# Weight factors of two up-projection blocks, made during the output projection and kept in DRAM; right factors made product by product

## The chip, the cores and the metric

The kernel runs on one core of one Trainium2 chip. The time is the device time of one execution, in microseconds; a kernel's time is the median of its runs.

## The reference

One layer of a hybrid decoder over 2048 tokens of width 1024, all in float32. A pooling mixer and a sliding-window attention are gated, added and projected by w_out onto the residual stream. Then comes the feed-forward part, which is what matters here:

```python
x = x + (g_pool * a + g_attn * b) @ w_out[l]
h = rmsnorm(x, ffn_norm[l])
up = causal_depthwise_conv(h @ w_up[l], conv_w[l], conv_b[l])   # 1024 -> 2 * 2816, width 3
gate, val = up[..., :D_FF], up[..., D_FF:]
x = x + (jax.nn.silu(gate) * val) @ w_down[l]
```

## The kernel before

**Halves and stages.** The tokens are worked in two halves (c = 0 and 1) of 1024. In each half come the mixer and the attention, the output projection (out_proj), the up-projection (up) with convolution and gate, and the down-projection. TensorE has no float32 product of its own here: each operand is split into a high part (a cast, on ScalarE) and a low part (a subtraction, on VectorE), and three matmuls (high x high, high x low, low x high) are added up in PSUM. mm3 does that for the projections, product for the up-projection.

**Up-projection.** There are 22 blocks f. A block is 128 gate columns and 128 value columns of w_up, and the whole is a 2x2 matrix of halves: gate and value against the two halves of the 1024 inputs on the left, inputs against the two halves (512) of the tokens on the right. It is multiplied by the scheme of Strassen and Winograd with seven products: A11 B11 (one), A12 B21 (two), S2 T2 (three), S1 T1 (four), S3 T3 (five), S4 B22 (six) and A22 T4 (seven). Each has 12 matmuls of 128 x 512 (four slices of the inputs, three parts). Up holds one block; its methods one to seven write the products into PSUM banks (tags f, a, t) and put them together: ScalarE copies a bank out (kept, tile Q) where a later one is added to it on VectorE.

**Left factors.** Blocks makes those of one block from its raw weights, in four steps: first gives A11 and A12, second A22, third S3 and S2, fourth S1 and S4, each by VectorE sums in place, a cast and a low part (L262 on VectorE and L261 on ScalarE for a full tile). The raw weights come through Stream, which loads three entries ahead of use (tiles R, three buffers) and parts the entry after next. w_out goes through the same Stream (L191 and L192 part its slabs), 16 slabs for two passes n over the token halves, and then the 22 blocks of w_up.

**Right factors.** xg holds x2 scaled by the norm's weight, in four tiles. The norm's own factor for a token half is known only when the squares of all eight row groups have been summed (rstd, L461 to L471), raised to a power on POOL (L464) and spread over the partitions (L480, L482). Half 0 is normed within the projection's second pass, and right_first makes B11 and B21 there. Half 1 is normed only in the up-projection's head: right_rest norms it (L865), forms the differences in place (L876 for T1, L882 for T2, L886 for T3, L889 for T4) and parts each factor (parted: L805 cast, L806 low part).

**Order.** The program is written as in the listing, but a scheduler places each instruction by its priority and by when its operands are ready, so engines work across these steps. SP issues all transfers from one queue in order. Buffers are few: tiles U 19, M 5, F 4, Q 4, R 3. In the head of up the order was: products one of blocks 0 and 1, spread, two of block 0, one of block 2, right_rest, two of blocks 1 and 2, then the loop over f, in which a block's products three to five are followed by six and seven of the block before.

Of the kernel before, what the change touches and what calls it, by code (L numbers as in the profile page):

```python
# [16 lines left out]
F32 = mybir.dt.float32  # L17
# [9 lines left out]
P = 128  # L27
# [16 lines left out]
MAGIC = 12582912.0  # L44
FOLD_FIRST = 5


# [77 lines left out]
def weight_order():  # L125
    out = []
    for c in range(NCH):
        if c > 0:
            out.append(("kv",))
        out += [(kind, j) for parts in first_fillers(c) for kind, j, n in parts if n == 0]  # L130
        out.append(("q", 0))
        for q4 in range(4):
            for n, parts in enumerate(fillers(c, q4)):
                if n == NB - 3 and q4 < 3:
                    out.append(("q", q4 + 1))
                out += [(kind, j) for kind, j, h in parts if h == 0]
        out += [("pg", ct) for ct in (6, 7)]
        out += [("out", m) for n in range(2) for m in range(KT)]
        out += [("up", f) for f in range(FT)]
        out += [("none", i) for i in range(3)]  # L140
    return out
# [23 lines left out]
def block_kernel(ctx: ExitStack, tc: tile.TileContext, x, xT, pos, vec, qkn, w_poolT, w_pool, w_q, w_kv,  # L165
# [66 lines left out]
    def split_weights(key, raws):  # L232
# [14 lines left out]
        return out if len(out) > 1 else out[0]  # L247

    class Blocks:

# [5 lines left out]
        def __init__(self, raws):  # L256
            self.raws, self.w, self.at = raws, {}, 0

        def halved(self, first, second, raw):
            t = up_.tile([P, 2, 8, P], F32R, "U")  # L260
            A.copy(t[:, 0], raw)  # L261
            V.tensor_sub(t[:, 1], raw, t[:, 0].bitcast(F32))  # L262
            self.w[first], self.w[second] = t[:, :, 0:4], t[:, :, 4:8]
# [10 lines left out]
        def second(self):  # L274
            g, v = self.raws
            t = mp.tile([P, 2, 4, P], F32R, "M")
            A.copy(t[:, 0], v[:, 4:8])
            V.tensor_sub(t[:, 1], v[:, 4:8], t[:, 0].bitcast(F32))
            self.w["A22"] = t
            V.tensor_sub(v[:, 0:4], g[:, 0:4], v[:, 0:4])  # L280
            V.tensor_sub(v[:, 4:8], v[:, 4:8], v[:, 0:4])  # L281
# [533 lines left out]
    def out_proj(c, ms):  # L815

        xg = [up_.tile([P, 2, T], F32, "U") for _ in range(4)]
        norms = []
        for n in range(2):
            acc = fp.tile([P, 512], F32, "F")  # L820
            c_ = slice(n * 512, (n + 1) * 512)
            for m in range(KT):
                xr = fp.tile([P, 512], F32, "F")
                load(xr, xT[m * P:(m + 1) * P, c * T + n * 512:c * T + (n + 1) * 512])
                w = stream.get("out", m)
                if n == 1 and m == 7:
                    stream.ahead().step(4)
                    stream.part(stream.used + 2)
                    stream.tiles[stream.used + 1].step(1)
                po = ps.tile([P, 512], F32, "f")  # L830
# [25 lines left out]
            norms += [stats, whole]  # L856
        return xg, b, norms[2:]

# [12 lines left out]

    def right_rest(xg, b, pb):
        for j in range(2):
            normed(xg[j], 1, pb)
            q11, q12 = xg[j][:, :, N0], xg[j][:, :, N1]
            V.tensor_sub(q11, q12, q11)  # L876
            b.setdefault("T1", []).append(parted(q11))
        t2s = []
        for j in range(2):
            normed(xg[j + 2], 1, pb)  # L880
            t2s.append(mp.tile([P, 2, 512], F32, "M"))
            V.tensor_sub(t2s[j], xg[j + 2][:, :, N1], xg[j][:, :, N0])  # L882
            b.setdefault("T2", []).append(parted(t2s[j]))
        for j in range(2):
            q12, q21, q22 = xg[j][:, :, N1], xg[j + 2][:, :, N0], xg[j + 2][:, :, N1]
            V.tensor_sub(q12, q22, q12)  # L886
            b.setdefault("T3", []).append(parted(q12))
            b.setdefault("B22", []).append(parted(q22))
            V.tensor_sub(q21, q21, t2s[j])  # L889
            b.setdefault("T4", []).append(parted(q21))  # L890
# [12 lines left out]
    class Up:  # L903
# [27 lines left out]

        def four(self):
            self.z = ps.tile([P, 512], F32, "t")
            self.mul(self.z, "S1", "T1", first=True)
# [33 lines left out]

        def gate(self):
            yg = self.conv(self.f, self.ug)  # L970
            t = mp.tile([P, T], F32, "M")
# [4 lines left out]

    def up(c, xg, b, norms, dn):
        units = [Up(c, f, b, None) for f in range(FT)]

# [6 lines left out]

        weights(0, 4)
        units[0].one()
        norms[0]()
        weights(1, 1)  # L990
        units[1].one()
        pb = norms[1]()
        units[0].two()
        weights(2, 1)
        units[2].one("t")
        right_rest(xg, b, pb)
        units[1].two()
        units[2].two()
        for f in range(FT + 1):
            u = units[f] if f < FT else None  # L1000
            old = units[f - 1] if f > 0 else None
            if u and f > 2:
# [6 lines left out]
            weights(f + 1, 1)  # L1009
            if old:  # L1010
                old.seven()
                old.value()
            weights(f + 1, 1)
            if f == 0:
                u.four()
            if u:
# [3 lines left out]
            weights(f + 1, 1)  # L1020
            if old:
                old.six()
                old.gate()
            weights(f + 1, 1)
            if f > 0 and u:
                u.four()
            if u:
                u.five()
# [296 lines left out]
```

## Time and profile before

| | |
|---|---|
| runs | 2494.67, 2495.66, 2496.61 us; median 2495.66 |
| the profiled execution | 2497.94 us, its span 2495.9, granted clock 0.995 |
| TensorE busy | 98% of the span |
| VectorE, ScalarE, POOL busy | 79%, 48%, 9% |
| DMA | 229.86 MB, 92 GB/s over the span |
| first half: output projection, head of up, block 2 on | from about 538, 624.4, 666.6 us |
| second half: head of up | from 1843.7 us |

The span is what the profile covers; the 2.0 us by which the execution's time exceeds it lie around it. Rows of the profile name engines as PE (TensorE matmul), PEld (its weight loads), DVE (VectorE), ACT (ScalarE), POOL and SP; L865 is line 865 of the listing. out<-in gives the names of the tiles without their numbers. The granted clock (PEclk) is 1.00 at 2.4 GHz and 0.50 at 1.2 GHz.

### The profile page before, as it was taken

Reading aid. Unit: us, or ns where it says so; the run is one execution under the profiler, and the core shown is the slowest. Engines: PE = TensorE matmul, PEld = TensorE weight load, DVE = VectorE, ACT = ScalarE, POOL = GpSimd, SP = SyncE. Lnnn points to the kernel's source line nnn. Section 1 sums busy time; section 2 is a strip of 40 time slices with the busy share of each in tenths; the row PEclk is TensorE's granted clock in tenths of the full one; section 3 lists DMA queues with packets and bytes.
Section 4 is the critical chain, followed back from the end, with each engine's and each line's share of the span. In section 5 each row is a group of like instructions: output and inputs, shape, how many; then the busy total and the mean of one; then the engine's idle time right before and its main releaser. Section 6 shows DMA issues by size and latency. Waiting matters only on the chain.

```text
span 2495.9 us, 32928 instructions
## 1 busy us (share of the span) xinstructions
PE 2438.3 (98%) x12224; PEld 2056.6 (82%) x12224; DVE 1982.5 (79%) x3544; ACT 1189.0 (48%) x2350; POOL 223.5 (9%) x217
## 2 busy tenths in 40 slices
PE   6999999999999999999999999999999999999999
PEld 6888888878788888788889888887877888887887
DVE  8786777876988788799857767779589788788994
ACT  6444444544554555543524444444445555454432
POOL 0121222200000000000002322222000000000000
PEclk9999999999999999999999999999999999999999
DMA  6221111035122233445221011100522222218321
GB/s 244 98 85 35 35 43 43 26 97 169 64 85 91 78 110 118 165 173 185 92 103 35 26 43 43 43 26 26 186 93 85 85 76 90 88 68 278 122 82 51
DMA packets 86991, 229.86 MB, mean 92 GB/s; under 512 B 9264, under 2 KB 11568, under 8 KB 86832
## 3 DMA queue, kind: packets, MB, share of 16 engines
q1 hardware_dynamic: 86832, 227.77, 26.8%
q8 instruction: 96, 1.57, 0.3%
q14 instruction: 63, 0.52, 0.1%
HBM read 183.69 MB, written 44.04 MB: 91 GB/s over the span
## 4 chain that ended last, share of the span: by engine, by line
PE 77%; DVE 14%; issue 3%; ACT 3%; DMA 2%; POOL 0%; SPq 0%; POOLq 0%; DVEq 0%; ACTq 0%
PE f L207 19%; PE f L896 17%; PE t L896 9%; PE a L207 6%; PE f L1166 4%; PE a L1166 4%; PE a L896 4%; PE s L1166 4%; PE t L1166 4%; DVE U L806 1%; ACT Q L677 1%; PE a L710 1%; PE s L656 1%; DVE F L760 1%; DVE U L192 1%
## 5 line engine op out<-in xcount | busy, mean ns | idle before, releaser
L207 PE MATMUL f<-U,U 128*128 128x512 f32 x3072 | 719.3, 391 | 7.4 <-ACT U L191 4.2
L207 PEld LDWEIGHTS f<-U,U 128*128 128x128 f32 x3072 | 570.6, 188 | 127.1 <-ACT U L191 6.7
L896 PE MATMUL f<-U,U 128*128 128x512 f32 x1512 | 366.4, 393 | 7.0 <-ACT U L805 2.3
L896 PEld LDWEIGHTS f<-U,U 128*128 128x128 f32 x1512 | 285.8, 189 | 71.4 <-ACT U L805 4.4
L962 DVE SCALAR_TENSOR_TENSOR M<-F,vc,M 128x1024 f32<-128x1024 f32 x176 | 225.1, 1282 | 130.5 <-ACT M L959 130.2
L896 PE MATMUL t<-U,U 128*128 128x512 f32 x1128 | 268.3, 391 | 2.9 <-ACT U L805 2.6
L207 PE MATMUL a<-U,U 128*128 128x256 f32 x1920 | 250.0, 286 | 14.1 <-ACT U L191 12.2
L207 PEld LDWEIGHTS a<-U,U 128*128 128x128 f32 x1920 | 242.9, 193 | 21.6 <-ACT U L191 12.2
L896 PEld LDWEIGHTS t<-U,U 128*128 128x128 f32 x1128 | 211.7, 188 | 50.2 <-ACT U L805 4.1
L677 ACT ACTIVATE Q<-s,st,r 128x128 f32<-128x128 f32 x256 | 114.3, 453 | 175.4 <-DVE st L672 167.6
L261 ACT CAST U<-R 128x1024 fp32r<-128x1024 f32 x132 | 137.9, 1054 | 64.8 <-DVE R L281 32.7
L569 POOL TENSOR_TENSOR r<-r,mhalf 128x4 f32<-128x4 f32 (+1 forms) x80 | 77.2, 966 | 950.0 <-DVE r L568 888.3
L262 DVE TENSOR_TENSOR U<-R,U 128x1024 fp32r<-128x1024 f32 x132 | 161.0, 1222 | 0.0
L192 DVE TENSOR_TENSOR U<-R,U 128x512 fp32r<-128x512 f32 x214 | 146.2, 712 | 16.8 <-ACT U L191 15.8
L191 ACT CAST U<-R 128x512 fp32r<-128x512 f32 x214 | 123.0, 619 | 42.6 <-PE f L207 27.2
L896 PE MATMUL a<-U,U 128*128 128x512 f32 x528 | 128.4, 390 | 0.0
L896 PE MATMUL f<-U,M 128*128 128x512 f32 x504 | 123.6, 394 | 3.7 <-DVE F L940 3.7
L1125 ACT CAST U<-U 128x1024 fp32r<-128x1024 f32 x74 | 77.2, 1051 | 86.2 <-PE a L1166 27.2
L896 PEld LDWEIGHTS f<-U,M 128*128 128x128 f32 x504 | 95.5, 190 | 24.9 <-DVE F L940 5.0
L896 PEld LDWEIGHTS a<-U,U 128*128 128x128 f32 x528 | 98.7, 188 | 20.3
L948 ACT COPY F<-f 128x512 f32<-128x512 f32 x42 | 24.8, 590 | 179.1 <-PE f L896 179.1
L959 ACT ACTIVATE M<-F,vc 128x1024 f32<-128x1024 f32 x88 | 109.3, 1244 | 1.3
(243 smaller groups left out, 3903.3 us busy)
## 6 DMA issues: line engine op xcount, KB each, us to landing
R<-w_up SPq DMA_DIRECT2D x88, 512.0 KB, 3.3
actd<-M SPq DMA_DIRECT2D x44, 512.0 KB, 2.6
U<-w_down SPq DMA_DIRECT2D x88, 256.0 KB, 5.3
U<-actd SPq DMA_DIRECT2D x88, 256.0 KB, 5.4
R<-w_out SPq DMA_DIRECT2D x32, 512.0 KB, 3.9
R<-w_ga SPq DMA_DIRECT2D x16, 512.0 KB, 3.3
R<-w_q SPq DMA_DIRECT2D x16, 512.0 KB, 3.3
R<-wfold SPq DMA_DIRECT2D x16, 512.0 KB, 3.3
```

The lines of the kernel that those rows point to most:

```text
L191: A.copy(hi[:, t], src[:, t])
L192: V.tensor_sub(lo[:, t], src[:, t], hi[:, t].bitcast(F32))
L207: nc.tensor.matmul(out, a, b, start=(i == 0), stop=(i == n - 1))
L261: A.copy(t[:, 0], raw)
L262: V.tensor_sub(t[:, 1], raw, t[:, 0].bitcast(F32))
L569: G.tensor_tensor(r, r, mhalf[:, 0:nh], op=ALU.pow)
L677: A.activation(pr[:, h, :], sc[:, h, 0:P], AF.Exp, bias=nm[:, h:h + 1], scale=it["rq"][:, h:h + 1], accum_out=rs[:, h:h + 1])
L896: nc.tensor.matmul(bank, a[:, x, k, :], b[k // 2][:, y, k % 2, :], start=(first and i == 0), stop=(i == 11), skip_group_check=True)
L959: A.activation(y, u[:, 2:], AF.Identity, bias=cw[:, 3, m:m + 1], scale=cw[:, 2, m:m + 1])
L962: V.scalar_tensor_tensor(y, u[:, j:j + T], cw[:, j, m:m + 1], y, op0=ALU.mult, op1=ALU.add)
L1125: A.copy(hi, src)
L1166: nc.tensor.matmul(into[m], u[:, 0, c_], v[:, 1], start=(first and j == 0), stop=(k == n - 1 and j == 2), skip_group_check=True)
```

## The change

Blocks 0 and 1 (PRE, with the row groups 0 and 4 at which they begin) leave the Stream. In the first pass of the first output projection their raw weights are loaded into a tile U, and Blocks makes all four of their tiles there, two steps at each of the next two row groups; at the third, store writes the tiles (high and low parts, 3.5 MiB a block) to DRAM. In the head of up of both halves the new class Kept loads these tiles back: A11 and A12 in the second pass of the output projection, the others at the points given in up. So the second half makes no left factors of these two blocks at all. right_rest is cut into right_t1, right_t2, right_t3, right_b22 and right_t4, which up calls in this order between the products: one of blocks 0, 1; two of 0, one of 2 (T1), two of 1 and 2 (T2), four of 0 (T3), three of 0, four of 1 (B22), five of 0 (T4), six and seven of 0, three and five of 1. The loop over f begins with block 2.

```diff
+PRE = {0: 0, 1: 4}
+
+
 V_AN = 0
...
         out += [("out", m) for n in range(2) for m in range(KT)]
-        out += [("up", f) for f in range(FT)]
+        out += [("up", f) for f in range(FT) if f not in PRE]
         out += [("none", i) for i in range(3)]
...
+    kept = {}
+
+    class Kept:
+
+
+        def __init__(self, f):
+            self.f, self.w = f, {}
+
+        def fetch(self, *names):
+            i = PARTS.index(names)
+            src = kept[self.f][i]
+            p, tag = (mp, "M") if names == ("A22",) else (up_, "U")
+            t = p.tile(list(src.shape), F32R, tag)
+            load(t.bitcast(F32), src)
+            for j, name in enumerate(names):
+                self.w[name] = t[:, :, 4 * j:4 * j + 4]
+
+        def step(self, n=1):
+            pass
+
+    PARTS = [("A11", "A12"), ("A22",), ("S3", "S2"), ("S1", "S4")]
+
     class Blocks:
...
             self.raws, self.w, self.at = raws, {}, 0
+            self.tiles = []
+
+        def store(self, f):
+            kept[f] = []
+            for i, t in enumerate(self.tiles):
+                kept[f].append(dp.tile(list(t.shape), F32, f"kept_{f}_{i}"))
+                load(kept[f][-1], t.bitcast(F32))
...
             t = up_.tile([P, 2, 8, P], F32R, "U")
+            self.tiles.append(t)
             A.copy(t[:, 0], raw)
...
             self.w["A22"] = t
+            self.tiles.append(t)
             V.tensor_sub(v[:, 0:4], g[:, 0:4], v[:, 0:4])
...
         norms = []
+        heads = [Kept(f) for f in PRE]
         for n in range(2):
...
                 w = stream.get("out", m)
+                for f, at in PRE.items() if c == n == 0 else ():
+                    if m == at:
+                        raw = up_.tile([P, 2, 8, P], F32, "U")
+                        load(raw[:, 0], w_up[f])
+                        load(raw[:, 1], w_up[FT + f])
+                        made = Blocks([raw[:, 0], raw[:, 1]])
+                    elif at < m < at + 3:
+                        made.step(2)
+                    elif m == at + 3:
+                        made.store(f)
+                if n == 1 and m >= 6:
+                    heads[m - 6].fetch("A11", "A12")
                 if n == 1 and m == 7:
-                    stream.ahead().step(4)
-                    stream.part(stream.used + 2)
-                    stream.tiles[stream.used + 1].step(1)
+                    stream.ahead().step(1)
                 po = ps.tile([P, 512], F32, "f")
...
             norms += [stats, whole]
-        return xg, b, norms[2:]
+        return xg, b, norms[2:], heads
...
-    def right_rest(xg, b, pb):
+    def right_t1(xg, b, pb):
         for j in range(2):
...
             b.setdefault("T1", []).append(parted(q11))
+
+    def right_t2(xg, b, pb):
+
         t2s = []
...
             b.setdefault("T2", []).append(parted(t2s[j]))
+        return t2s
+
+    def right_t3(xg, b):
         for j in range(2):
-            q12, q21, q22 = xg[j][:, :, N1], xg[j + 2][:, :, N0], xg[j + 2][:, :, N1]
+            q12, q22 = xg[j][:, :, N1], xg[j + 2][:, :, N1]
             V.tensor_sub(q12, q22, q12)
             b.setdefault("T3", []).append(parted(q12))
-            b.setdefault("B22", []).append(parted(q22))
+
+    def right_b22(xg, b):
+        for j in range(2):
+            b.setdefault("B22", []).append(parted(xg[j + 2][:, :, N1]))
+
+    def right_t4(xg, b, t2s):
+        for j in range(2):
+            q21 = xg[j + 2][:, :, N0]
             V.tensor_sub(q21, q21, t2s[j])
...
-        def four(self):
-            self.z = ps.tile([P, 512], F32, "t")
+        def four(self, tag="t"):
+            self.z = ps.tile([P, 512], F32, tag)
             self.mul(self.z, "S1", "T1", first=True)
...
-        def gate(self):
-            yg = self.conv(self.f, self.ug)
+        def gate(self, yg=None):
+            if yg is None:
+                yg = self.conv(self.f, self.ug)
             t = mp.tile([P, T], F32, "M")
...
-    def up(c, xg, b, norms, dn):
-        units = [Up(c, f, b, None) for f in range(FT)]
+    def up(c, xg, b, norms, heads, dn):
+        units = [Up(c, f, b, heads[f] if f < 2 else None) for f in range(FT)]
...
-        weights(0, 4)
-        units[0].one()
+
+        u0, u1, u2 = units[:3]
+        u0.one()
         norms[0]()
-        weights(1, 1)
-        units[1].one()
+        u1.one()
         pb = norms[1]()
-        units[0].two()
+        u0.two()
+        weights(2, 0)
+        u2.one("t")
+        for u in (u0, u1):
+            u.w.fetch("S1", "S4")
+        u0.w.fetch("S3", "S2")
+        right_t1(xg, b, pb)
+        u1.two()
+        u2.two()
+        t2s = right_t2(xg, b, pb)
+        u0.four()
+        u0.w.fetch("A22")
+        right_t3(xg, b)
+        u0.three()
+        u1.four("a")
+        right_b22(xg, b)
+        u0.five()
+        u1.w.fetch("S3", "S2")
+        right_t4(xg, b, t2s)
         weights(2, 1)
-        units[2].one("t")
-        right_rest(xg, b, pb)
-        units[1].two()
-        units[2].two()
-        for f in range(FT + 1):
+        u0.six()
+        yg = u0.conv(0, u0.ug)
+        u0.seven()
+        u0.value()
+        weights(2, 1)
+        u1.w.fetch("A22")
+        u1.three()
+        u0.gate(yg)
+        weights(2, 1)
+        u1.five()
+        for f in range(2, FT + 1):
             u = units[f] if f < FT else None
-            old = units[f - 1] if f > 0 else None
+            old = units[f - 1]
             if u and f > 2:
...
             weights(f + 1, 1)
-            if old:
-                old.seven()
-                old.value()
+            old.seven()
+            old.value()
             weights(f + 1, 1)
-            if f == 0:
-                u.four()
             if u:
...
             weights(f + 1, 1)
-            if old:
-                old.six()
-                old.gate()
+            old.six()
+            old.gate()
             weights(f + 1, 1)
-            if f > 0 and u:
+            if u:
                 u.four()
-            if u:
                 u.five()
```

On SP the four stores of block 0 stand among the stores of x2 of row groups 1 to 3 of the first pass, and those of block 1 among groups 5 to 7; behind block 0's stand loads of xT and w_out and the raw weights of block 1. In the head of the first half the loads run: A11/A12 of block 0, the gate part of block 3's w_up, x2, A11/A12 of block 1, S1/S4 of 0, x2, S1/S4 of 1, S3/S2 of 0, A22 of 0, S3/S2 of 1, A22 of 1, then the value part of block 3.

The first place is VectorE in the head of the first half, from the statistics of token half 1 (r, L461 before, L495 now) on; R is raw weights, s the spread factor, U_5845 to U_5848 are xg. Before:

```order
L461 TENSOR_SCALAR r_15_204<-a_6574 128x4
L280 TENSOR_TENSOR R_6501<-R_6499,R_6501 128x512
L480 COPY M_6612<-r_15_204 128x512
L278 TENSOR_TENSOR M_6589<-R_6501,M_6589 128x512
L281 TENSOR_TENSOR R_6501<-R_6501 128x512
L288 TENSOR_TENSOR R_6499<-R_6499,R_6501 128x512
L289 TENSOR_TENSOR R_6499<-R_6499,R_6501 128x512
L865 TENSOR_TENSOR U_5845<-U_5845,s_6611 128x2x512
L926 TENSOR_TENSOR F_6557<-a_6618,Q_6572 128x512
L262 TENSOR_TENSOR U_6636<-R_6553,U_6636 128x1024
L876 TENSOR_TENSOR U_5845<-U_5845 128x2x512
L865 TENSOR_TENSOR U_5846<-U_5846,s_6611 128x2x512
```

Now, from the same place on:

```order
L495 TENSOR_SCALAR r_15_204<-a_6612 128x4
L514 COPY M_6641<-r_15_204 128x512
L910 TENSOR_TENSOR U_5845<-U_5845,s_6640 128x2x512
L910 TENSOR_TENSOR U_5846<-U_5846,s_6640 128x2x512
L921 TENSOR_TENSOR U_5845<-U_5845 128x2x512
L984 TENSOR_TENSOR F_6595<-a_6647,Q_6610 128x512
L921 TENSOR_TENSOR U_5846<-U_5846 128x2x512
L840 TENSOR_TENSOR U_6690<-U_5845,U_6690 128x1024
L910 TENSOR_TENSOR U_5847<-U_5847,s_6640 128x2x512
L840 TENSOR_TENSOR U_6695<-U_5846,U_6695 128x1024
L984 TENSOR_TENSOR F_6623<-a_6698,Q_6638 128x512
L930 TENSOR_TENSOR M_6727<-U_5847,U_5845 128x1024
```

The weight operations (L262 to L289) have gone from between the right factors; two tiles are normed before the first difference, and the low parts of T1 (L840) follow with only norms and sums of products (L984) between them.

The second place is VectorE in the first pass of the first output projection, around the residual add (L834 before, L879 now) of row group 5; R is slabs of w_out, F_5849 sums the squares. Before:

```order
L192 TENSOR_TENSOR U_6057<-R_6014,U_6057 128x512 x2
L192 TENSOR_TENSOR U_6098<-R_6055,U_6098 128x512 x2
L834 SCALAR_TENSOR_TENSOR M_6087<-f_6062,F_6053 128x512
L493 TENSOR_TENSOR F_5849<-F_5849,M_6090 128x512
L834 SCALAR_TENSOR_TENSOR M_6128<-f_6103,F_6094 128x512
L493 TENSOR_TENSOR F_5849<-F_5849,M_6131 128x512
```

Now (U_6048 is the raw weights of block 1):

```order
L195 TENSOR_TENSOR U_6087<-R_6041,U_6087 128x512 x2
L295 TENSOR_TENSOR U_6092<-U_6048,U_6092 128x1024
L314 TENSOR_TENSOR U_6048<-U_6048 128x512
L311 TENSOR_TENSOR M_6095<-U_6048,M_6095 128x512
L879 SCALAR_TENSOR_TENSOR M_6125<-f_6100,F_6083 128x512
L315 TENSOR_TENSOR U_6048<-U_6048 128x512
L322 TENSOR_TENSOR U_6048<-U_6048 128x512
L323 TENSOR_TENSOR U_6048<-U_6048 128x512
L527 TENSOR_TENSOR F_5849<-F_5849,M_6128 128x512
L195 TENSOR_TENSOR U_6136<-R_6085,U_6136 128x512 x2
```

Of the block's making, one low part and two half-size operations now stand ahead of that add, and three more between it and the low part of the slab for row group 7, which before stood ahead of the add.

## Rows read from the trace of the kernel before

**Rows 1.** The page: the span, and the busy time of each engine.

```profile
span 2495.9 us, 32928 instructions
...
PE 2438.3 (98%) x12224; PEld 2056.6 (82%) x12224; DVE 1982.5 (79%) x3544; ACT 1189.0 (48%) x2350; POOL 223.5 (9%) x217
```

**Rows 2.** Stage windows: stretch, us, busy time of each engine, PEclk, DMA share, GB/s.

```profile
538.00:582.00 44.00, 43.10 (x189) 35.40 (x190) 23.91 (x37) 21.09 (x38) 0.00 (x0) 1.00 0.66 207
624.40:666.60 42.20, 37.55 (x155) 28.64 (x154) 39.84 (x43) 20.36 (x27) 1.40 (x1) 0.88 0.11 37
666.60:720.00 53.40, 53.40 (x236) 43.90 (x235) 48.02 (x53) 31.07 (x48) 0.00 (x0) 1.00 0.30 104
1843.70:1885.90 42.20, 37.10 (x155) 27.65 (x154) 39.83 (x43) 20.17 (x26) 1.40 (x1) 0.92 0.11 38
```

**Rows 3.** The chain of waits from 620 to 670 us, its shares by line.

```profile
by line: DVE U L806 20.9%; PE f L896 17.0%; PE f L207 9.5%; DVE U L865 7.1%; issue 5.4%; DVE M L882 4.7%; DVE U L262 4.6%; DVE U L886 4.5%; DVE U L889 4.5%; DVE U L876 4.5%; PE a L471 3.2%; POOL r L464 2.8%; DVE F L926 2.6%; PE a L896 2.5%;
```

**Rows 4.** TensorE's timeline, first half: start, us, instruction, count, idle before and releaser.

```profile
624.38 2.88 PE L896 MATMUL f<-U,U 128*128 128x512 f32 x12
627.10 0.28 PE L471 MATMUL a<-one,F 128*128 128x1 f32 x2
...
628.93 0.28 PE L471 MATMUL a<-one,M 128*128 128x1 f32 x2
...
630.41 1.17 PE L896 MATMUL a<-U,U 128*128 128x512 f32 x4
...
633.69 1.05 PE L482 MATMUL s<-identr,M 128*128 128x128 f32 x8
634.50 1.17 PE L896 MATMUL a<-U,U 128*128 128x512 f32 x4
...
647.43 0.50 PE L896 MATMUL f<-U,U 128*128 128x512 f32 x1 [0.77 <-ACT U L805]
...
650.91 0.79 PE L896 MATMUL f<-U,U 128*128 128x512 f32 x1 [0.75 <-ACT U L805]
...
666.60 1.77 PE L896 MATMUL f<-U,M 128*128 128x512 f32 x7
```

**Rows 5.** Timelines of POOL, VectorE and ScalarE in the same stretch.

```profile
630.83 1.40 POOL L464 TENSOR_TENSOR r<-r,mhalf 128x4 f32<-128x4 f32 x1 [37.84 <-DVE r L461]
...
632.26 0.43 DVE L480 COPY M<-r 128x512 f32<-128x512 f32 x1 [0.90 <-POOL r L464]
...
636.39 0.68 DVE L926 TENSOR_TENSOR F<-a,Q 128x512 f32<-128x512 f32 x1
636.99 1.22 DVE L262 TENSOR_TENSOR U<-R,U 128x1024 fp32r<-128x1024 f32 x1
638.12 1.22 DVE L876 TENSOR_TENSOR U<-U 128x1024 f32<-128x1024 f32 x1
...
639.38 1.05 ACT L805 CAST U<-U 128x1024 fp32r<-128x1024 f32 x1 [3.95 <-DVE U L876]
```

**Rows 6.** DMA issues: out<-in, queue, count, KB each, us from issue to landing.

```profile
R<-w_up SPq DMA_DIRECT2D x88, 512.0 KB, 3.3
...
U<-x2d SPq DMA_DIRECT2D x8, 1024.0 KB, 7.1
```

**Rows 7.** Two windows of five microseconds in the first output projection.

```profile
545.00:550.00 5.00, 5.00 (x24) 4.14 (x23) 1.49 (x3) 1.24 (x2) 0.00 (x0) 1.00 0.86 306
555.00:560.00 5.00, 5.00 (x24) 4.14 (x23) 1.94 (x3) 1.25 (x2) 0.00 (x0) 1.00 0.86 254
```

**Rows 8.** TensorE's timeline at the start of the first output projection.

```profile
538.29 0.73 PE L207 MATMUL f<-U,U 128*128 128x512 f32 x2 [1.77 <-ACT U L191]
539.63 2.56 PE L207 MATMUL f<-U,U 128*128 128x512 f32 x10 [0.61 <-DVE U L192]
```

**Rows 9.** VectorE's timeline in the same projection.

```profile
566.72 0.69 DVE L834 SCALAR_TENSOR_TENSOR M<-f,F 128x512 f32<-128x512 f32 x1 [0.33 <-PE f L207]
```

**Rows 10.** A window of ten microseconds in the head.

```profile
650.00:660.00 10.00, 7.24 (x16) 4.82 (x16) 10.00 (x10) 6.62 (x8) 0.00 (x0) 0.50 0.00 0
```

## Prediction

> **What bounds the kernel now.** I read the page first: TensorE is busy for 98% of the span [rows 1], so only stretches in which it waits can give time back. Next I cut the span into stage windows [rows 2]. In the stretch after the up-projection of block 2 has begun, TensorE is busy without a gap (53.40 of 53.40 us). In the head of the up-projection it is busy for 37.55 of 42.20 us at a granted clock of 0.88, while VectorE is busy for 39.84 of 42.20. The second half of the sequence shows the same (37.10 of 42.20). The chain of waits inside that stretch [rows 3] is a string of VectorE operations on L806, L865, L876, L882, L886 and L889, those of right_rest, with TensorE (f, L896) at 17%. So VectorE makes the right factors too late there, and the reader should see that the head is the one large place where TensorE starves.
>
> **What the head costs.** Twelve matmuls take 2.72 us (624.38 to 627.10, [rows 4]), so one takes 0.2267. From 624.38 to 666.60 the program has 130 matmuls of the up-projection, which is 29.5 us, the small ones of the statistics (twice 0.28 in rows of two; those of the last groups run on to 630.41; 1.6 together) and the spreading (633.69 to 634.50, 0.8): 31.9 us. It takes 42.2. The loss is 10.3 us, and the same stretch of the second half is as long, with as many matmuls in it [rows 2]: again 10.3. The most that the change can give in the heads is therefore 20.6 us.
>
> **The head after.** I set zero at the first matmul of the up-projection. A full-size VectorE operation (128x1024) is followed by the next after 1.13 us and lasts 1.22, a half-size one is followed after 0.60; a full-size cast on ScalarE takes 1.05 [rows 5].
> - Products. Block 0's first product ends at 2.7, the statistics at 4.5. VectorE, POOL (1.40) and the copy that follows give the row to spread at about 6.8 [rows 5]. TensorE does block 1's first product until 7.2 and spreads until 8.0. Then four products (seconds of blocks 0, 1, 2, first of 2) need nothing new and run until 18.9. The squares that the statistics need came within 4.5 us here even with weight making around them (627.10 and 628.93, [rows 4]); that is gone, so I count no wait, 1.8 us at most (4.5 less 2.7).
> - VectorE from 8.3 on. The first part of T1 needs five full-size operations and one half-size one: 8.3 + 4 x 1.13 + 0.6 + 1.2 = 14.6; the second two more, 16.9. TensorE wants them at 18.9: no wait, and this was the first late factor before. T2's first part is ready at 21.7, wanted at 21.8. T2's second part comes four operations later, 26.3, wanted at 25.9: 0.4 lost. The fifth product may start only when ScalarE has copied the third out of the bank. That copy stands behind five casts that begin at 23.0, so it ends at 28.7; TensorE is there at 27.7: 1.0 lost. T3 (28.5), B22 (30.9) and T4 (34.9 and 36.7) are there within 0.1 of when they are wanted.
> - Sum of waits: 1.5 us instead of 10.3. Bounds: 0, and 3.9 if each of some 30 operations takes the full 1.22 and not 1.13. Per head 8.8 us are won (6.4 to 10.3); for two, 17.6 (12.8 to 20.6).
> - The last factor load (S3/S2 of block 1) goes into the buffer that T3 frees, so it starts at 27.5 and is wanted at 34. Such a 1024 KB load took 7.1 us where others ran beside it; half the size took 3.3 [rows 6], so alone it should take about 5. I count nothing; up to 0.7 per head.
> - The weights of blocks 2 and 3 come later in SP's queue than before, behind those loads. By the same count block 3's second half lands at about 45 and is wanted at 50: nothing.
>
> **The first output projection of the first half.** Here the two blocks are made: per block three full-size and five half-size VectorE operations (6.4 us) and 3.7 us of ScalarE casts. Both engines have the room: VectorE is busy 23.91 and ScalarE 21.09 of 44 us there [rows 2]. What has no room is the DMA. It moves 207 GB/s there at a share of 0.66 (9.1 MB); the change adds 2 MiB of raw weights and 7 MiB of stores, 18.5 MB in all. One five-microsecond slice shows 306 GB/s at 0.86, another 254 at the same share [rows 7], so the full rate lies between 295 and 356; I take 330. From 546.6 on SP issues four stores of block 0, three stores of x2, one load of xT, one of w_out and then the raw weights of block 1: 6 MiB, 19.1 us; with 0.8 for the start, an estimate (512 KB take 3.3 us from issue to landing [rows 6], their bytes alone 1.6), these land at 566.5. On SP the stores wait for the last low part of their block, and behind them stand the next stores of x2 and loads of w_out, which TensorE needs two groups later.
>
> The Trainium skill (DMA: Bandwidth & Descriptors, "Where 436 GB/s comes from") gives about 358 GB/s as what the memory grants one core; the better slice agrees. By that figure the load would land 1.5 us earlier and the term below would be about 1.1 instead of 2.6.
>
> TensorE leaves a group every 24 x 0.2267 = 5.44 us; group 1 (counted from 0) begins at 539.6 [rows 8], so group 6 ends at 572.3. VectorE's low part of block 1 waits for that load and stands ahead of the residual add of group 5. That add began at 566.72 and was done at 567.4 [rows 9]; behind a cast, that low part and two half-size operations it is done at 570.9. ScalarE's two operations on it end at 572.2, and only then come the casts of the w_out slab for group 7: TensorE waits 1.2 us. The next slab stands behind two more casts and adds: 1.0. A third stands behind the statistics of the first half: 0.4. Sum 2.6 us lost, once. Bounds: 0 if the load lands at 565, 6 if it lands 3.4 us later than I say. In the second half nothing is made there: 0.
>
> **Sum.** The profiled execution took 2497.9 us (span 2495.9 and 2.0 around it). 2497.9 - 17.6 + 2.6 = 2482.9. It lies 2.3 above the median of the runs, 2495.7, so I forecast 2480.7, rounded to 2481.
>
> **The rivals.**
> 1. The clock still falls. In the old head it was granted 0.50 for ten microseconds (1.2 GHz) [rows 10] after three gaps of 0.75 to 0.77, the first at 647.43 and the last at 650.91 [rows 4]. In the new one, gaps of 0.4 and 1.0 lie close together. Against it: gaps of 1.77 and 0.61 at 538 to 539.6 left the clock at 1.00 [rows 2, 8]. Ten microseconds at half clock cost 5 per head: 2481 + 10 = 2491. The Trainium skill (TensorE: Matmul & The Clock Gate, "A second HAM failure mode: psum-queue depth-cycling") says that frequent short gaps between groups suffice for the clock to swing; that is this rival, and the old head agrees with it.
> 2. The whole half of the projection runs at the DMA's pace. 18.5 MB at 356 GB/s are 52 us, 8 more than the 44; then 8 are lost and not 2.6: 2486. For it: SP has one queue, and loads of w_out stand behind the stores. Against it: the last stores need not be done by then.
> 3. All waits go and the projection keeps its pace: 2495.7 - 20.6 = 2475.
> 4. Slower than before: the stores halve the DMA's rate. At 165 GB/s the 6 MiB take 38 us, 19 more, and block 1's raw weights hold up VectorE and ScalarE, and so every later slab, by that time: 2480.7 + 19, about 2500. It decides from a rate below some 170 GB/s on. No busy slice shows less than 254 at 0.86 [rows 7], and x2 stores are among them.
> 5. The change doesn't do what it says: the factors come back from DRAM later than VectorE made them before. Block 0's first load is issued nine microseconds before it is wanted, the others four and more; only the 27.5 one is near. It would cost some 2 per head: 2485, inside the range.
>
> **How the numbers follow.** Forecast 0.50 (its own range 2476 to 2487), rival 1 0.13, rival 2 0.14, rival 3 0.10, rival 4 0.06, rival 5 0.04, others 0.03. The range 2474 to 2492 leaves out rival 4, the upper part of rival 1, and the others. A difference below 0.2%, 5 us, can't be told from none: that line is 2490.7. Same 0.10 (half of rival 1, which stands on that line, and the others), slower 0.06 (rival 4), faster 0.84 (the rest).
>
> **What would show it.** In the profile after: the head's window 34 us long and not 42, at clock 1.00; TensorE's waits on L806 gone, and a wait of about 1 us on ScalarE's copy Q in their place; in the first output projection waits of about 1 us on the w_out casts near 572 and 579; DMA share near 0.9 from 552 to 590. Wrong if these waits reach 6 us, if the clock shows 0.50 in the head, or if TensorE waits there on a load of kept factors.

## The result and the profile after

The changed kernel takes 2481.09 us (median of 4 runs, 2479.70 to 2486.34) against 2496.14 us (median of 4, 2494.67 to 2500.41). The medians are 15.0 us apart. The ratio on record, 0.9948 with a 95% interval of [0.9936, 0.9959], stands for about 13 us; it is not the quotient of the medians, 0.9940, which lies inside the interval. A second set of five runs gave 2479.23 us and 0.9938 [0.9926, 0.9951].

The page of the changed kernel, span and busy time, answers to [rows 1]:

```profile
span 2484.5 us, 32982 instructions
...
PE 2433.9 (98%) x12224; PEld 2056.0 (83%) x12224; DVE 1967.4 (79%) x3528; ACT 1181.0 (48%) x2342; POOL 222.5 (9%) x217
```

The profiled execution is the slowest of the four (2486.34 us). To see where its 11.4 us of span come from I cut it at the same pieces of work: from the gap at the start of the first output projection to the first matmul of the up-projection, and from there to the 130th. The columns are those of [rows 2].

```profile
538.82:631.08 92.26, 89.56 (x384) 72.33 (x385) 61.43 (x86) 45.42 (x74) 1.01 (x1) 0.96 0.82 281
631.08:664.51 33.43, 32.76 (x156) 26.94 (x155) 26.34 (x27) 14.40 (x21) 1.01 (x1) 1.00 0.40 160
1841.65:1875.35 33.70, 32.89 (x156) 27.03 (x155) 26.38 (x28) 14.32 (x20) 1.01 (x1) 1.00 0.41 159
...
578.00:590.00 12.00, 12.00 (x54) 9.65 (x53) 4.84 (x8) 4.56 (x8) 0.00 (x0) 1.00 1.00 382
```

The same stretch of the output projection before the change:

```profile
538.29:624.38 86.09, 85.08 (x385) 70.23 (x385) 50.14 (x73) 39.80 (x68) 1.01 (x1) 1.00 0.58 183
```

The heads take 33.4 and 33.7 us instead of 42.2 each [rows 2], 8.8 and 8.5 won. VectorE is busy there for 26.3 us and not 39.8. The output projection takes 6.2 us more. The rest, 0.2 us won, is what the other stretches leave: 0.5 us more ahead of the projection and 0.8 less behind the second head.

In the head the timelines of VectorE, ScalarE and TensorE (start, us, instruction, idle before and releaser) can be laid on the prediction's sums, with zero at 631.08:

```profile
639.46 2.35 DVE L910 TENSOR_TENSOR U<-U,s 128x1024 f32<-128x1024 f32 x2 [2.06 <-PE s L516]
...
646.87 1.22 DVE L840 TENSOR_TENSOR U<-U,U 128x1024 fp32r<-128x1024 f32 x1
...
656.01 1.21 DVE L840 TENSOR_TENSOR U<-M,U 128x1024 fp32r<-128x1024 f32 x1
...
655.03 4.03 ACT L839 CAST U<-U 128x1024 fp32r<-128x1024 f32 x4
658.97 0.58 ACT L972 COPY Q<-f 128x512 f32<-128x512 f32 x1
...
659.60 2.78 PE L954 MATMUL f<-U,U 128*128 128x512 f32 x11 [0.67 <-ACT Q L972]
```

Norming starts at 8.4 (8.3 forecast), the second part of T1 is done at 17.0 (16.9), that of T2 at 26.1 (26.3). The one wait left is the forecast one: TensorE stands 0.67 us before product five until ScalarE, behind its row of casts, has copied product three. The forecast had 1.0, and 0.4 for T2 that did not come.

The output projection has two new waits, on the low part of a w_out slab and on a cast of a later one, and two falls of the granted clock. First TensorE, VectorE and SP's queue, then two windows:

```profile
540.16 34.96 PE L210 MATMUL f<-U,U 128*128 128x512 f32 x144 [0.61 <-DVE U L195]
575.73 5.99 PE L210 MATMUL f<-U,U 128*128 128x512 f32 x24 [0.61 <-DVE U L195]
...
594.93 15.00 PE L210 MATMUL f<-U,U 128*128 128x512 f32 x57 [0.94 <-ACT U L194]
...
565.16 0.69 DVE L879 SCALAR_TENSOR_TENSOR M<-f,F 128x512 f32<-128x512 f32 x1 [4.49 <-DMA F<-xT]
...
592.40 0.69 DVE L879 SCALAR_TENSOR_TENSOR M<-f,F 128x512 f32<-128x512 f32 x1 [8.25 <-DMA R<-w_out]
...
583.36 1.22 SPq L188 DMA_DIRECT2D F<-xT  x1
```

```profile
542.00:546.00 4.00, 4.00 (x15) 3.20 (x14) 2.70 (x4) 4.00 (x8) 0.00 (x0) 0.71 0.96 316
594.00:598.00 4.00, 3.07 (x8) 2.16 (x9) 2.66 (x5) 2.44 (x5) 1.01 (x1) 0.69 0.91 249
```

Idle time of the stretch is 2.7 us (92.26 less 89.56) against 1.0 before, so 1.7 are waits. The other 4.5 are matmuls that took longer: 144 that should take 32.65 us took 34.96, and 57 took 15.00 where the thin-stores kernel below, at clock 1.00, needs 13.21.

Both waits go back to adds (L879) that stood still for x^T. The add of row group 4 stood 4.49 us until 565.16, and from there to the low part of the slab for row group 7 (575.00) VectorE, with block 1's making among its work, has no break longer than 1.3 us. No operation of VectorE or ScalarE waited for block 1's raw weights. The add at 592.40 stood 8.25 us. Its row names a load of w_out, but the two such loads that were issued next, at 584.6 and 585.9, landed only at 593.4 and 594.7. What landed at 592.3 is its operand from x^T, asked for at 583.4, behind 3.5 MiB of kept stores, while the DMA moved 382 GB/s at a share of 1.00 (578 to 590 above). On ScalarE the cast that TensorE waits for stands behind this add's result. Its slab, the first of those two loads, was late too: it landed 0.9 us before the cast began.

### The profile page after: what moved, and what is told of

Its sections match the earlier page's. It is cut to its first block, busy times and chain, and to the rows that moved or that the text cites. A ratio compares the mean times of both kernels' runs of the same rounds, so it can differ in the third digit from the quotient of the medians.

```text
span 2484.5 us, 32982 instructions
## 1 busy us (share of the span) xinstructions
PE 2433.9 (98%) x12224; PEld 2056.0 (83%) x12224; DVE 1967.4 (79%) x3528; ACT 1181.0 (48%) x2342; POOL 222.5 (9%) x217
## 4 chain that ended last, share of the span: by engine, by line
PE 79%; DVE 13%; ACT 3%; DMA 2%; issue 2%; SPq 0%; POOL 0%; DVEq 0%; ACTq 0%; POOLq 0%
PE f L210 20%; PE f L954 18%; PE t L954 9%; PE a L210 6%; PE a L954 4%; PE f L1244 4%; PE a L1244 4%; PE t L1244 4%; PE s L1244 4%; ACT Q L711 1%; PE a L744 1%; PE s L690 1%; DVE F L794 1%; DVE U L195 1%; DVE U L840 1%
## 5 line engine op out<-in xcount | busy, mean ns | idle before, releaser
L210 PEld LDWEIGHTS a<-U,U 128*128 128x128 f32 x1920 | 242.4, 192 | 20.9 <-ACT U L194 11.3
L954 PE MATMUL t<-U,U 128*128 128x512 f32 x1080 | 254.2, 389 | 0.0
L954 PEld LDWEIGHTS t<-U,U 128*128 128x128 f32 x1080 | 202.7, 188 | 42.1
L294 ACT CAST U<-R 128x1024 fp32r<-128x1024 f32 x120 | 125.4, 1053 | 65.9 <-DVE R L315 33.9
L295 DVE TENSOR_TENSOR U<-R,U 128x1024 fp32r<-128x1024 f32 x120 | 146.6, 1222 | 0.5 <-ACT U L294 0.5
L194 ACT CAST U<-R 128x512 fp32r<-128x512 f32 x214 | 123.2, 619 | 41.1 <-PE f L210 27.8
L954 PE MATMUL a<-U,U 128*128 128x512 f32 x576 | 138.6, 389 | 0.0
L954 PEld LDWEIGHTS a<-U,U 128*128 128x128 f32 x576 | 108.0, 188 | 22.3
```

The source lines that it names most:

```text
L194: A.copy(hi[:, t], src[:, t])
L210: nc.tensor.matmul(out, a, b, start=(i == 0), stop=(i == n - 1))
L954: nc.tensor.matmul(bank, a[:, x, k, :], b[k // 2][:, y, k % 2, :], start=(first and i == 0), stop=(i == 11), skip_group_check=True)
```

## The experiments

In each set the kernel before ran on the same chip (medians 2495.4, 2496.13 and 2494.93 us).

**The changed kernel again**, no edit.

> The changed kernel once more, unchanged, for its spread and for a second trace. In the first trace (2486.3 us, 5 us above its other three runs) the first output projection is 6.2 us longer than before: new waits of 0.61 and 0.94 us, and some 4.2 us in stretches with a granted clock of about 0.7 (at 542 to 546 and 594 to 602). My theory: the heads gain 8.7 us each in every execution; the clock's falls in the output projection are not in every execution, so that this trace has one of them or none and a time of 2480 to 2482. Rival: the falls belong to the change (they follow its new waits) and show again at the same places; then the profiled time lies again near 2486.

2479.23 us, 0.9938 [0.9926, 0.9951]. The traced execution took 2483.92 us; its output projection:

```profile
538.40:628.38 89.98, 87.62 (x384) 71.12 (x385) 61.25 (x86) 45.47 (x74) 1.01 (x1) 0.98 0.82 287
...
540.00:544.00 4.00, 4.00 (x19) 3.27 (x19) 2.78 (x5) 3.08 (x5) 0.00 (x0) 1.00 0.65 185
592.00:596.00 4.00, 3.68 (x9) 2.68 (x10) 2.64 (x5) 1.83 (x4) 0.84 (x1) 0.58 0.86 245
```

Heads 33.4 us each, as in the first trace. The fall at 540 is gone, that at 592 is there again (0.58), so the stretch is 2.3 us shorter. Both theories are half right: one fall comes and goes, the one behind the new wait came twice.

**The order alone.** PRE is empty, the blocks are made as before the change, and the order is the new one:

```diff
-PRE = {0: 0, 1: 4}
+PRE = {}
...
+        weights(0, 4)
         u0.one()
         norms[0]()
+        weights(1, 1)
         u1.one()
...
         right_t3(xg, b)
+        weights(1, 3)
         u0.three()
```

> Only the order of right factors and products as in the change; the left factors of blocks 0 and 1 are made as before (block 0 and a part of block 1 at the end of the output projection, the rest in the head), nothing is kept in DRAM. My theory: both parts are needed, since the making of block 1 still stands between the right factors on VectorE (two full-size low parts ahead of B22 and T4, half-size sums ahead of the norms): of the 8.7 us a head gains with both, the order alone gives some 4 to 5, and the output projection loses nothing: 2496 - 9, about 2487 (2484 to 2490). Rival A (order is all): 2479, below the changed kernel, since the stores' cost is saved. Rival B (VectorE's load is all): 2495 to 2497.

2493.93 us, 0.9991 [0.9982, 1.0000]. The heads:

```profile
624.24:664.80 40.56, 36.06 (x156) 28.06 (x155) 37.16 (x40) 20.53 (x28) 1.40 (x1) 0.92 0.17 59
1842.23:1883.05 40.82, 35.88 (x156) 28.01 (x155) 37.16 (x40) 20.32 (x27) 1.40 (x1) 0.92 0.18 58
```

1.7 and 1.4 us won, not 4 to 5. VectorE still has 37.2 us to do in a head that takes 33.4 in the changed kernel. My expectation (2484 to 2490) was wrong in size: it counted the operations between the factors, not that their sum is more than the head.

**The kept blocks alone.** right_rest is put back whole, with products in about the old order:

```diff
-        right_t1(xg, b, pb)
+        u0.w.fetch("A22")
+        right_rest(xg, b, pb)
         u1.two()
         u2.two()
-        t2s = right_t2(xg, b, pb)
         u0.four()
...
         u0.three()
-        u1.four("a")
-        right_b22(xg, b)
         u0.five()
```

> Only the other part: the left factors of blocks 0 and 1 are made in the first output projection and kept in DRAM as in the change, but the right factors come in the old order (T3, B22 and T4 of one tile together) and the products in about the old order. My theory: T1 and T2 are as early as in the change, but the second part of T3 comes behind both other factors of the first tile, some 3.4 us later than TensorE wants it, and T2's second part 1.8 late: waits of 6 to 7 us per head in place of 10.3, 3.5 to 4 us gained per head (more if the clock stays up), less 2 for the output projection: about 2490 (2486 to 2493). Rival B (VectorE's load is all): as the changed kernel, 2481.

2493.49 us, 0.9989 [0.9980, 0.9998]. Output projection and first head:

```profile
538.86:628.80 89.94, 87.57 (x385) 71.31 (x385) 61.16 (x86) 45.69 (x74) 1.01 (x1) 0.98 0.82 288
...
628.80:667.61 38.81, 35.34 (x156) 28.03 (x155) 31.51 (x34) 15.91 (x23) 1.01 (x1) 0.96 0.38 152
```

The heads gain 3.4 and 3.9 us (38.81 and 38.29), as expected; the projection loses 3.9 and not 2, so the time is just above the stated range. VectorE's load now fits (31.5 us) but T3's second part comes behind other factors. The parts give 1.7 and 3.4 us in the first head alone and 8.8 together: one takes away the load, the other the wrong order, and either limit alone holds the head. Neither rival (order alone, load alone) stands.

**Thin stores.** Only the first tile of each block is stored, 2 MiB and not 7, and all loads read it. So blocks 0 and 1 are multiplied by wrong factors; the instructions and their sizes stay:

```diff
-            for i, t in enumerate(self.tiles):
-                kept[f].append(dp.tile(list(t.shape), F32, f"kept_{f}_{i}"))
-                load(kept[f][-1], t.bitcast(F32))
+            t = self.tiles[0]
+            kept[f].append(dp.tile(list(t.shape), F32, f"kept_{f}"))
+            load(kept[f][-1], t.bitcast(F32))
...
-            src = kept[self.f][i]
+            src = kept[self.f][0][:, :, 0:4 * len(names)]
```

> The change with its stores cut from 7 MiB to 2: of each block only the tile of A11 and A12 is stored, and every load of the heads reads that one (as many bytes loaded as in the change; the products of blocks 0 and 1 use wrong factors). All making of factors on VectorE and ScalarE is as in the change. My theory: the new wait of 0.94 us in the second pass comes from loads of x^T that stand behind the stores; it goes, and with it a fall of the clock where there was one; the 0.61 stays or goes with the earlier raw weights: 1 to 2 us below the changed kernel, 2479 to 2480, and the add L879 waits no more for 8 us. Rival: the cost of the first pass is the order on VectorE and ScalarE, and the time stays that of the changed kernel (within 0.5 us).

2476.61 us, 0.9926 [0.9913, 0.9940], 2.6 below the changed kernel on the same chip; I had expected 1 to 2.

```profile
537.11:623.25 86.14, 85.14 (x384) 70.22 (x385) 60.99 (x86) 45.63 (x74) 1.01 (x1) 1.00 0.71 240
```

The stretch is as long as before the change (86.09) with VectorE and ScalarE as busy as in the changed kernel (60.99 and 45.63 against 61.25 and 45.47). So the making costs nothing there, and the whole cost comes with the stores. This run takes away bytes and stores together; the next two part them from the place in the queue and from the time at which they come.

**Stores from another queue.**

```diff
-                load(kept[f][-1], t.bitcast(F32))
+                nc.gpsimd.dma_start(kept[f][-1], t.bitcast(F32))
```

> The change with its eight stores of kept tiles issued from POOL's queue and not from SP's; as many bytes, all else as in the change. The thin-stores kernel has shown that the stores' bytes cost the 2.6 us (2476.6 against 2479.2). Theory A: they cost by their place, since loads of x^T and w_out stand behind them in SP's one queue; from another queue those pass, the add L879 no longer waits 8 us for x^T, and the time is that of the thin stores, 2476 to 2478. Theory B: they cost by the bandwidth alone (the DMA moves 408 to 426 GB/s between 578 and 590); then the small loads are as late as before and the time stays at 2479 to 2480.

2482.34 us, 0.9948 [0.9935, 0.9961]: nothing won, 2 us above what theory B gave, and theory A falls. The add's wait of 8 us at 592 is gone, but TensorE has another. TensorE, then waits of VectorE and ScalarE in the projection (for what, us in total, times, longest):

```profile
569.37 24.50 PE L210 MATMUL f<-U,U 128*128 128x512 f32 x96 [3.61 <-ACT U L194]
...
ACT U L880 <- DVE M L879: 30.1, 11, 10.7
...
DVE U L314 <- DMA U<-w_up: 8.6, 1, 8.6
```

The cast that TensorE waits for stands on ScalarE behind L880, which waited 10.7 us for the add of row group 4. That add stands on VectorE behind a sum of block 1 (L314), which waited 8.6 us for the block's raw weights. They were asked for 8 us earlier than in the changed kernel (at 551.9 and not 560.1) and took 10 to 13 us to land instead of 7.5 to 8.3, while the DMA moved 398 GB/s (551.9 to 566.2). So the load that the prediction watched is the late one here. The clock was at 0.50 from 568 to 572, behind this gap, and the projection took 92.4 us. The stores cost by the bandwidth that they take, not by their place in the queue.

**The stores spread out.** Block 1 is made from row group 7 on, across the two passes:

```diff
-PRE = {0: 0, 1: 4}
+PRE = {0: 0, 1: 7}
...
-                for f, at in PRE.items() if c == n == 0 else ():
-                    if m == at:
+                for f, at in PRE.items() if c == 0 else ():
+                    i = 8 * n + m
+                    if i == at:
...
```

> The change with block 1 made later: its raw weights are loaded at row group 7 of the first pass and its tiles stored at row group 2 of the second, so that the stores of the two blocks lie some 38 us apart and not 22. Theory (the load of the DMA in the first pass sets the cost): the passes now carry about as many bytes each, the 8 us wait for x^T shrinks below the 5 us that a group lasts, and the time is 2477 to 2478. Rival: block 1's making then stands on VectorE ahead of the right factors of the second pass (right_first), the head begins late, and nothing is won: 2479 to 2482.

2478.41 us, 0.9933 [0.9921, 0.9946].

```profile
537.83:624.54 86.71, 85.31 (x384) 70.12 (x385) 61.35 (x86) 45.76 (x74) 1.38 (x1) 1.00 0.87 300
```

As many bytes, a higher share (0.87), and 86.7 us: 0.6 more than before the change. No add there waits for x^T longer than 3.9 us. Once more, beside the next two kernels:

> The spread kernel (block 1 made from row group 7 on) once more, unchanged, beside its filled form. Its first trace has the first output projection 86.7 us long, against 90.0 in the changed kernel's second trace and 86.1 before the change. Theory: this holds in every execution, and the time is 2477 to 2479 again.

2476.18 us, 0.9926 [0.9914, 0.9939], a little below what was expected, projection 86.8 us. This is the fastest whole version; its intervals overlap those of the changed kernel, but its projection is 3 to 5.5 us shorter in the traces.

**The old head with its gaps filled.** The kernel before, with matmuls by zero in block 0's products three and six:

```diff
+                for _ in range(fill.get(i, 0)):
+                    nc.tensor.matmul(bank[0:64], zero, ready[0][:, 0, 0, :], start=False, stop=False,
+                                     skip_group_check=True)
...
+            fill = {"S2": {0: 4, 1: 4, 6: 4}, "S4": {0: 6}}.get(x, {}) if self.f == 0 else {}
```

> The kernel before, with 18 more matmuls per head: they multiply by zero and are added into the banks of block 0's products three and six, at the places where TensorE waits there (4 ahead of product three, 4 between the high and the low part of its factor, 4 ahead of its second half, 6 ahead of product six). VectorE and ScalarE do what they did. Of the 8.8 us that a head is longer before than after the change, idle time is 4.0 and the rest is matmuls at the lower clock. Theory: the clock falls because of the gaps, so filled gaps keep it at 1.00 and a head gets shorter by up to 4.8 less some 0.5 for fill that outlasts its gap, though TensorE has 4.1 us more to do: 2495.4 - 8, about 2487 (2485 to 2491). Rival: the fall has nothing to do with the gaps, or the low clock costs nothing where VectorE sets the pace: 2495 to 2497, and 0.50 in the head again.

2496.80 us, 1.0004 [0.9995, 1.0014].

```profile
627.61:669.86 42.25, 38.60 (x174) 28.97 (x173) 39.89 (x43) 20.40 (x27) 1.40 (x1) 1.00 0.12 39
1845.07:1887.32 42.25, 38.60 (x174) 28.97 (x173) 39.88 (x43) 20.19 (x26) 1.40 (x1) 1.00 0.11 38
```

The clock stays at 1.00, and the head is 42.25 us long, as it was at 0.88 [rows 2]. So the gaps do bring the clock down, but here the low clock costs nothing: VectorE, busy for 39.9 us, sets the length, and a faster TensorE only waits longer. My theory was wrong on the time and right on the clock.

**Filled gaps where TensorE sets the pace.** Eleven matmuls by zero in front of row group 0 of each projection, in the spread and in the changed kernel (8 ahead of the first matmul, 3 ahead of the third):

```diff
+                    {0: 8, 2: 3} if n == m == 0 else {})
```

> The spread kernel with 11 matmuls by zero at the start of each output projection, 8 in the gap of 1.8 us and 3 in that of 0.6, where TensorE waits for the first slab of w_out. In some traces the granted clock falls to 0.6 to 0.8 for some 4 us behind these gaps (at 540 in the first trace after the change, at 1752 to 1760 in four of eight), which costs 2 us where TensorE sets the pace, unlike in the old head. Theory: with the gaps filled the fall there is gone in every execution; mean gain 0.5 to 2 us over the spread kernel: 2476 to 2478, and no clock below 1.00 from 536 to 548 and 1750 to 1762. Rival: the falls come also without a gap, or the fill costs as much as it gives: the time of the spread kernel within 0.5 us.

> The changed kernel with the same 11 matmuls by zero at the start of each output projection. Theory: as there, 0.5 to 2 us below the changed kernel's 2479 to 2481: 2478 to 2480, and no fall of the clock at 540 and 1756 in its trace; the fall behind the wait at 592 to 596 stays, since that wait stays.

2480.72 us, 0.9945 [0.9931, 0.9959], and 2482.54 us, 0.9951 [0.9939, 0.9964]: where a gain was expected the first is 4.5 us slower than the spread kernel of the same set, the second 1.5 to 3.3 above the changed kernel's two medians. TensorE in the first of the two:

```profile
533.92 2.00 PE L216 MATMUL f<-U,zero 128*64 128x512 f32 x8
535.76 0.62 PE L218 MATMUL f<-U,U 128*128 128x512 f32 x2
536.23 0.86 PE L216 MATMUL f<-U,zero 128*64 128x512 f32 x3
536.92 11.26 PE L218 MATMUL f<-U,U 128*128 128x512 f32 x47
```

The fill stands one row group too early: group 0 had no gap, the wait was at group 1, and it is now swallowed (47 matmuls without a stop). It costs 2.5 us for 2.4 saved in the first half and for 1.5 in the second. No fall shows at 540 or 1756 in either trace, but none shows there in the two traces of the spread kernel without a fill either. Falls show at 128 and at 1048 to 1056, and in the second also at 596. None of these is the fill's: of all twelve traces eight have a fall at 124 to 128, and five one at 1048 to 1060, that of the kernel before among them; the one at 596 shows in the changed kernel too.

Part of the rest was lost long before the fill. The first of the two kernels, then the spread kernel's second trace, in the first stages:

```profile
44.00:48.00 4.00, 2.48 (x22) 2.33 (x21) 3.27 (x8) 3.99 (x7) 0.00 (x0) 1.00 0.77 269
...
44.00:48.00 4.00, 3.91 (x33) 3.71 (x33) 4.00 (x16) 4.00 (x10) 0.00 (x0) 1.00 0.68 251
```

From 40 to 52 us TensorE waits 1.5 us for a cast (L194) in the first kernel and 1.6 in the second, and 2.0, in three waits, in the kernel before with its gaps filled; in the nine traces without a fill its timeline shows no wait there. So this came in with the fill's edit, which also makes a tile of zeros at the program's start; by what step is not shown. These runs therefore can't tell what a filled gap is worth where TensorE sets the pace. The reading of the old head stands, since it rests on the length of the head itself.

## Why the prediction was right

**The heads.** Forecast 8.8 us each, measured 8.8 and 8.5. The count of VectorE's operations gave the right times to 0.2 us, and the wait that stayed was the named one. The exact hit is in part luck: the new head is 1.5 us longer than the 31.9 us of work that were counted, as forecast, but only 0.7 of that is a wait; most of the other 0.9 are matmuls that took longer than 0.2267 us each. That the head is set by VectorE is shown three ways: filled gaps at full clock leave it at 42.25 us, less load alone gives 3.4 to 3.9, order alone 1.4 to 1.7.

**The output projection.** Forecast 2.6 us, measured 6.2 in the first trace and 3.9 in the second: this term was too small. Its cause, the DMA, was right (thin stores bring it to 0), but two steps were not. The waits are 1.6 us (0.61 and 0.94). The first came where it was worked out, on the slab for row group 7 and behind block 1's making. But what held that up was not block 1's raw weights, for which nothing waited in either trace; it was an add that stood 4.49 us for x^T behind block 0's stores. In the spread kernel, where block 1 is made later, the like add stands 3.9 us and TensorE does not stop. The second wait is an add that stands for x^T behind block 1's stores. The sum had no wait for x^T. And the falls of the clock behind gaps, which rival 1 put into the new heads, came here, where TensorE sets the pace and each costs about 2 us. A smaller slip: group 1 begins with the two matmuls at 538.29 [rows 8] and not at 539.6, so by the prediction's own count group 6 ends at 571.8. The rate itself was near, 330 GB/s taken and 328 measured from 552 to 590, at a share of 0.93 where about 0.9 was forecast; but the bound of 356 was too low, as 12 us show 382. By the Trainium skill (DMA: Bandwidth & Descriptors, "Where 436 GB/s comes from") about 358 is the ceiling for transfers between HBM and SBUF; the measurement differs, in a stretch of loads and stores together.

**The sum.** 2482.9 was forecast for a profiled execution and 2486.3 came; from there to the median I subtracted 2.3, and it was 5.2. The two errors have opposite signs, so the 0.1 us between 2481.0 and 2481.1 is luck; a hit within 3 us is what the terms support.

**The rivals.** 1: the clock did fall, but not in the heads, which ran at 1.00 with a 0.67 us gap. Its price, 5 us for ten at half clock, taken from the old head, was wrong there: that fall cost nothing. 2: the projection at the DMA's pace came nearest by the number, 6.2 and 3.9 for 8, but not as it was told: TensorE stopped twice, for 0.6 to 0.9 us, and lost most of the rest to the clock. 3 did not come, though the spread version, with 0.6 us in the projection, goes most of the way. 4 and 5: the rate did not drop, and no matmul in the heads waited for a kept tile.

## What to carry to other kernels

Before pricing a wait or a low clock, ask which engine sets that stretch: filling TensorE's gaps changed nothing in 42 us that VectorE ruled, while the same fall cost 2 us where TensorE ruled. When two limits stand together (load and order), try both at once, since each edit alone looks nearly worthless. Work moved off a full engine through DRAM is paid in DMA time where it lands: spread the stores over the stretch before looking for another queue.

## What the hardware showed

The granted clock falls behind some gaps of 0.6 to 1.8 us and not behind others: after the same gaps (1.76 and 0.61 us) at the start of the output projection it fell to 0.71 in one trace of the changed kernel and stayed at 1.00 in the other (0.71 is a mean over 4 us of the two levels, 1.2 and 2.4 GHz). Executions of one kernel differ by up to 8.7 us (2477.6 to 2486.3 over the changed kernel's nine). Beside those at the program's start and end, windows of 4 us show five falls in its first trace (2486.3 us), four in its second (2483.9) and none in that of the thin stores (2475.8), so a term of 2 us can't be read from one trace alone. The DMA moved 382 GB/s over 12 us, and 398 over 14 us with the stores on POOL's queue, loads and stores mixed.
